# Turning a decoder's input once, unscaled, and keeping it in DRAM for the first residual

## The chip, the core and the metric

One core of a Trainium2 chip runs the kernel. The metric is the device time of one execution in microseconds. Five engines work side by side, each through its own instructions in a fixed order: TensorE (PE: products and transposes into PSUM), VectorE (DVE), ScalarE (ACT), GpSimd (POOL) and SyncE (SP, which issues transfers). They meet by semaphores.

## What is computed

Two decoder layers, for 1024 prompt tokens and 8 sample tokens of 1024 features. The first layer's mixer is gated linear attention (GLA), the second's sliding-window attention; each layer has a squared-ReLU MLP, and each sub-layer is `h = h + post_norm(f(pre_norm(h)))`. What the change touches is the first sub-layer:

```
def rms_norm(x, g):
    return x * rsqrt(mean(x * x, axis=-1) + NORM_EPS) * g
def gla_mixer(x, s0, w_in, w_gate2, b_gate, g_head, w_out):
    q, k, v, r, z = split(x @ w_in)
    log_a = log_sigmoid(z @ w_gate2 + b_gate) / GLA_TAU
    o, s_new = gla_recurrence(q * GLA_DK_HEAD ** -0.5, k, v, log_a, s0)
    return (rms_norm(o, g_head) * silu(r)) @ w_out, s_new
hp = hp + rms_norm(gla_mixer(rms_norm(hp, norm_mix_pre[0]), ...), norm_mix_post[0])
```

The factor `rsqrt(...)` is one number per token, the gain `g` one per feature.

## The kernel before

Activations lie with features on partitions. The tokens form two groups: A (prompt blocks 0 to 3 and the samples, N = 520, in chunks of 256 and 264) and B (blocks 4 to 7, N = 512). Everything but the attention's inner work is a linear layer, cut into jobs: one job is a column tile of 128 of a weight matrix. Weights and activations are split into a high and a low part (fp32r), and a product is three: `wh xh`, `wh xl`, `wl xh` (L217, L219, L221, the tile `psl`). `prep` (L195 to L205) loads a tile in two halves of 256 KB into three staging buffers `wst`, ScalarE casts the high part `wh`, VectorE subtracts for `wl`; it runs one job ahead. `psl` has three PSUM buffers, all else (`aux`) five.

Around the jobs, `Task` objects hold background work (norms, attention, loading); `tick` emits a step of them when so many us of products have gone by. A scheduler then sets each engine's order from the emitted program, by its own estimates, except for instructions kept in program order by `tc.keep_in_program_order`.

`load_x` (L414 to L478) loads the input by blocks of 128 tokens, tokens on partitions: squares and their sum on ScalarE (L438), the factor with one Newton step (L441 to L446, `xss`), the scaling by factor and gain on VectorE (L449; the gain, broadcast over partitions, is loaded at L467), eight transposes on TensorE (L459, `xT`) and the split into the two parts (L289, L290). For group A this runs at the start, with `wz` (the 16 gate columns) and two weight tiles among it; group B's runs as background task `tB`. `gla_part1` then makes `z` and `r` (copied from PSUM at L511 to `sr`), `gla_gate` the decays `eq` and `ek`, `gla_head` the keys, queries and values of a head (`qd` L585, `ki` L589, copy of `vT` L593), `gla_inner` its recurrence. In `gla_inner` the samples' states are updated (L704, `s`, from the product `pkv` L701), split (`sh` on ScalarE, `sl` on VectorE), and multiplied with the queries (L695, `pso`), collected by `so` (L715) and the product of L719.

The residual: `norms` adds, tile by tile, what `residual` gives. `from_scratch` (L353) reads it from `xs`, a DRAM copy that the norm before has written. The first norms use `from_input` (L356 to L373): load 256 KB of the input, four transposes (L364, `pxi`), for A one of the samples (L371, `pxs`), and an addition from PSUM (L366).

## Time and profile before

| | |
|---|---|
| median of 3 runs | 2284.32 us (2284.18 to 2285.45) |
| span of the profiled execution | 2282.3 us |
| TensorE busy | 2255.3 us |
| VectorE busy | 1463.2 us |
| ScalarE busy | 1230.0 us |
| GpSimd busy | 81.7 us |

The span is measured inside the profiled execution, from its first to its last instruction; the runs' times are 2.0 us longer. Busy times are sums over an engine's instructions; an idle engine's row names the instruction or transfer that ended the idle time.

### The profile page before, as it was taken

The page shows a single profiled execution, that of the slowest core. Times are in us where ns is not written, and L with a number is a line of the kernel's source. Part 1 is how long each engine was busy: PE and PEld are TensorE (multiplying, and loading weights), DVE is VectorE, ACT ScalarE, POOL GpSimd, SP SyncE. Part 2 cuts the span into 40 slices and gives each one's busy share as a digit, 9 for nine tenths or more (in the row PEclk, how much of TensorE's full clock was granted, in tenths as well). Part 3 has the DMA queues.
Part 4 walks back from the last instruction along what each step waited for, and adds up shares of the span by engine and source line. Part 5 has one row for each costly group of instructions (what it writes and reads, how often), then busy time and mean ns, then how long its engine had stood idle before and what let it go on. Part 6 is the DMA issues. An engine that isn't in the chain of part 4 may idle for free.

```text
span 2282.3 us, 39657 instructions
## 1 busy us (share of the span) xinstructions
PE 2255.3 (99%) x14764; PEld 2053.8 (90%) x14764; DVE 1463.2 (64%) x3186; ACT 1230.0 (54%) x2614; POOL 81.7 (4%) x121
## 2 busy tenths in 40 slices
...
GB/s 169 128 132 92 105 78 77 126 138 155 93 93 93 90 92 172 97 110 93 79 86 77 103 157 131 131 111 77 75 75 78 93 163 110 171 105 97 93 97 83
DMA packets 413634, 246.75 MB, mean 108 GB/s; under 512 B 17817, under 2 KB 400889, under 8 KB 412641
## 3 DMA queue, kind: packets, MB, share of 16 engines
...
q8 instruction: 116, 1.90, 0.4%
...
## 4 chain that ended last, share of the span: by engine, by line
PE 95%; DVE 2%; DMA 1%; ACT 1%; issue 0%; POOL 0%; ACTq 0%; DVEq 0%; POOLq 0%
PE psl L219 29%; PE psl L217 29%; PE psl L221 29%; PE psc L978 1%; PE ppt L1007 1%; PE po L1018 1%; PE po L1019 1%; PE pP L657 1%; PE pO L684 0%; PE pO L682 0%; PE pxi L364 0%; PE pvt L629 0%; PE patt L633 0%; DMA cm<-const_cmask_dram 0%; DVE nxn L334 0%
## 5 line engine op out<-in xcount | busy, mean ns | idle before, releaser
L217 PE MATMUL psl<-xh,wh 128*128 128x512 f32 (+2 forms) x2784 | 890.8, 320 | 0.7 <-ACT sr L511 0.3
L221 PE MATMUL psl<-xh,wl 128*128 128x512 f32 (+2 forms) x2784 | 886.0, 318 | 1.8 <-DVE xss L445 1.7
L219 PE MATMUL psl<-xl,wh 128*128 128x512 f32 (+2 forms) x2784 | 886.6, 319 | 0.0
L204 ACT CAST wh<-wst 128x512 fp32r<-128x512 f32 x712 | 440.9, 620 | 717.1 <-PE psl L219 629.7
L205 DVE TENSOR_TENSOR wl<-wst,wh 128x512 fp32r<-128x512 f32 x712 | 497.5, 700 | 347.2 <-ACT wh L204 310.9
L221 PEld LDWEIGHTS psl<-xh,wl 128*128 128x128 f32 x2784 | 523.3, 188 | 39.1 <-DVE wl L205 2.4
L217 PEld LDWEIGHTS psl<-xh,wh 128*128 128x128 f32 x2784 | 524.1, 188 | 37.6 <-ACT sr L511 0.6
L219 PEld LDWEIGHTS psl<-xl,wh 128*128 128x128 f32 x2784 | 523.9, 188 | 35.8
L221 PE MATMUL psl<-hh,wl 128*128 128x256 f32 (+2 forms) x1536 | 487.3, 317 | 0.0
L217 PE MATMUL psl<-hh,wh 128*128 128x256 f32 (+1 forms) x1504 | 479.6, 319 | 0.0
L219 PE MATMUL psl<-hl,wh 128*128 128x256 f32 (+1 forms) x1504 | 479.2, 319 | 0.0
L221 PEld LDWEIGHTS psl<-hh,wl 128*128 128x128 f32 x1536 | 288.9, 188 | 20.5
L217 PEld LDWEIGHTS psl<-hh,wh 128*128 128x128 f32 x1504 | 283.0, 188 | 20.8 <-ACT hh L289 0.3
L219 PEld LDWEIGHTS psl<-hl,wh 128*128 128x128 f32 x1504 | 282.7, 188 | 20.7 <-DVE hl L290 0.3
L793 DVE TENSOR_TENSOR yf<-yf,psl 128x256 f32<-128x256 f32 (+1 forms) x344 | 172.4, 502 | 151.7 <-PE psl L221 150.2
L290 DVE TENSOR_TENSOR hl<-rl,hh 128x256 fp32r<-128x256 f32 (+1 forms) x192 | 98.8, 515 | 144.5 <-ACT hh L289 144.4
L780 ACT ACTIVATE rl<-psl 128x256 f32<-128x256 f32 (+1 forms) x192 | 87.1, 454 | 63.1 <-PE psl L221 57.5
L781 ACT ACTIVATE rl<-rl 128x256 f32<-128x256 f32 (+1 forms) x192 | 94.5, 492 | 4.6
L289 ACT CAST hh<-rl 128x256 fp32r<-128x256 f32 (+1 forms) x192 | 92.3, 481 | 4.7
L305 DVE TENSOR_TENSOR nacc<-nacc,nsq 128x520 f32<-128x520 f32 (+1 forms) x99 | 68.6, 693 | 17.3 <-ACT nsq L304 15.0
L992 ACT ACTIVATE pb<-pb,mx 128x256 f32<-128x256 f32 (+1 forms) x128 | 62.2, 487 | 5.7 <-DVE mx L990 4.7
L984 DVE CUSTOM_DVE_ANT_0 pb<-psc,smask 128x256 f32<-128x256 f32 (+1 forms) x128 | 47.8, 401 | 1.2 <-PE psc L978 1.1
...
## 6 DMA issues: line engine op xcount, KB each, us to landing
wst<-in_ffn_w_up_dram SPq DMA_DIRECT2D x256, 256.0 KB
wst<-in_ffn_w_down_dram SPq DMA_DIRECT2D x256, 256.0 KB
...
```

Of the source, the lines that this page charges most:

```text
L204: nc.scalar.copy(out=wh[:, :, :m], in_=st[:, :, :m])
L205: nc.vector.tensor_tensor(out=wl[:, :, :m], in0=st[:, :, :m], in1=r(wh[:, :, :m]), op=ALU.subtract)
L217: nc.tensor.matmul(o, lhsT=wh[:, k % 4, :m], rhs=xh[:, k, c0:c0 + n], start=(k == 0), stop=False)
L219: nc.tensor.matmul(o, lhsT=wh[:, k % 4, :m], rhs=xl[:, k, c0:c0 + n], start=False, stop=False)
L221: nc.tensor.matmul(o, lhsT=wl[:, k % 4, :m], rhs=xh[:, k, c0:c0 + n], start=False, stop=(k == kt - 1))
L289: nc.scalar.copy(out=h, in_=src)
L290: nc.vector.tensor_tensor(out=l, in0=src, in1=r(h), op=ALU.subtract)
L305: nc.vector.tensor_tensor(out=acc, in0=acc, in1=sq, op=ALU.add)
L780: nc.scalar.activation(out=rl, in_=ps, func=AF.Relu)
L781: nc.scalar.activation(out=rl, in_=rl, func=AF.Square)
L793: nc.vector.tensor_tensor(out=o, in0=o, in1=ps, op=ALU.add)
L992: nc.scalar.activation(out=pb[:, i, k0:], in_=pb[:, i, k0:], func=AF.Exp, bias=mx[:, i:i + 1], accum_out=st[:, 2 + i:3 + i])
```

## The change

The input is turned as it is, in pairs of blocks, four PSUM tiles of 128x2x256 to a pair. The gain, now one number per partition (`g1`), is applied as the tiles leave PSUM. Group B multiplies by the factor there too (`rsB`: the factors of 256 tokens on all partitions, by a product of ones with a diagonal matrix `dg` into `prs`). Group A does not: its products with `w_in` are made from the unscaled input, and the factors `rsA` are multiplied afterwards: into `z`, `sr` and `vT` as they leave PSUM, on VectorE, and into `eq` and `ek` on GpSimd, which carries them into queries and keys. `keep` copies each turned tile from PSUM (ScalarE) and writes it to `xs` in DRAM, from ScalarE's queue for A and from GpSimd's for B; `from_input` is gone, and the first norms read their residual from there. `wz` comes in one transfer, the gate's weights later, and several casts and subtractions are kept in program order. Comments were removed as well. The core of the diff, blank lines left out:

```diff
+    g8 = const.tile([KT, P], F32, name="g8")
+    nc.scalar.dma_start(out=g8, in_=n_mix_pre[0].rearrange("(k p) -> k p", p=P))
+    g1 = const.tile([P, KT], F32, name="g1")
+    pg = aux([P, KT], "pg")
+    nc.tensor.transpose(pg, g8, ident[:KT, :KT])
+    nc.vector.tensor_copy(out=g1, in_=pg)
 ...
     def prep_z(w, col0, pin=False):
         wz = gp.tile([P, KT, 2 * RANK], F32R, tag="wz", name="wz", bufs=1)
-        for hf in range(2):
-            st = wpool.tile([P, 4, P], F32, tag="wst", name="wst", bufs=WS)
-            nc.sync.dma_start(out=st[:, :, :RANK], in_=w[hf * 512:hf * 512 + 512, col0:col0 + RANK].rearrange(
+        st = wpool.tile([P, 4, P], F32, tag="wst", name="wst", bufs=WS)
+        st = st.rearrange("p a b -> p (a b)")[:, :KT * RANK].rearrange("p (k m) -> p k m", m=RANK)
+        nc.sync.dma_start(out=st, in_=w[:, col0:col0 + RANK].rearrange("(k p) m -> p k m", p=P))
+        wh, wl = wz[:, :, :RANK], wz[:, :, RANK:]
+        pinned(nc.scalar.copy(out=wh, in_=st), pin)
+        pinned(nc.vector.tensor_tensor(out=wl, in0=st, in1=r(wh), op=ALU.subtract), pin)
         return wz
 ...
-    def from_input(y, g):
-        def add_x(k):
-            xt = npool.tile([P, 4, P], F32, tag="nt", name="nxi", bufs=3)
-            nc.scalar.dma_start(out=xt, in_=x_prompt[0, g.b0 * P:(g.b0 + 4) * P, k * P:(k + 1) * P].rearrange(
-                "(n p) d -> p n d", p=P))
-            pt = aux([P, 4, P], "pxi")
-            for n in range(4):
-                nc.tensor.transpose(pt[:, n, :], xt[:, n, :], ident)
 ...
-                ps = aux([P, NS], "pxs")
-                nc.tensor.transpose(ps, xm, ident[:NS, :NS])
-                nc.vector.tensor_tensor(out=y[:, k, TB:TB + NS], in0=y[:, k, TB:TB + NS], in1=ps, op=ALU.add)
-        return add_x
-    def norms(g, gpost, gpre, box, residual=from_scratch):
+    def norms(g, gpost, gpre, box):
         y = g.y
-        yield from post_norm(y, g, gpost, residual(y, g))
 ...
-    gbc, xtk = scr[:, 0:D], scr[:, 3 * D:4 * D]
+    rsA, rsB, xsm = scr[:, 0:NMAX], scr[:, NMAX:NMAX + 256], scr[:, NMAX + 256:D]
+    xtk = [scr[:, D:2 * D], scr[:, 3 * D:4 * D]]
 ...
-    def load_x(g, box, tiles, early=None):
 ...
-            for hf in range(2):
-                c = slice(hf * 512, hf * 512 + 512)
-                nc.vector.scalar_tensor_tensor(out=t[:, c], in0=t[:, c], scalar=y, in1=gbc[:rows, c],
-                                               op0=ALU.mult, op1=ALU.mult)
 ...
+    def load_x(g, h, l, pair, tiles):
+        own = g.i == 0
+        c0 = pair * 256
+        ns = g.ns if pair == 1 else 0
+        def pin(ins):
+            return pinned(ins, own)
+        for i in range(2):
+            row = (g.b0 + 2 * pair + i) * P
+            nc.sync.dma_start(out=tiles[i], in_=x_prompt[0, row:row + P, :])
+        if ns:
+            nc.sync.dma_start(out=tiles[2][:NS], in_=x_sample[:, 0, :])
+        yield YD
+        ss = gp.tile([P, 12], F32, tag="xss", name="xss", bufs=4)
+        if ns:
+            nc.gpsimd.memset(ss, 1.0)
+        n = 3 if ns else 2
+        def squares(i):
+            rows = P if i < 2 else NS
             jk = gp.tile([P, D], F32, tag="Sp", name="xsq", bufs=1)
+            sq = nc.scalar.activation(out=jk[:rows], in_=tiles[i][:rows], func=AF.Square,
+                                      accum_out=ss[:rows, i:i + 1])
+            if i:
+                pin(sq)
+        def factors():
+            ms, y, u = ss[:, 3:3 + n], ss[:, 6:6 + n], ss[:, 9:9 + n]
+            nc.vector.tensor_scalar(out=ms, in0=ss[:, 0:n], scalar1=1.0 / D, scalar2=EPS, op0=ALU.mult, op1=ALU.add)
             nc.scalar.activation(out=y, in_=ms, func=AF.Ln)
             nc.scalar.activation(out=y, in_=y, func=AF.Exp, scale=-0.5)
+            nc.vector.tensor_tensor(out=u, in0=y, in1=ms, op=ALU.mult)
+            nc.vector.tensor_tensor(out=u, in0=u, in1=y, op=ALU.mult)
             nc.vector.tensor_scalar(out=u, in0=u, scalar1=-0.5, scalar2=1.5, op0=ALU.mult, op1=ALU.add)
             nc.vector.tensor_tensor(out=y, in0=y, in1=u, op=ALU.mult)
+            N = 256 + ns
+            dg = nt(N, "dg")
+            for i in range(2):
+                nc.vector.tensor_scalar_mul(dg[:, i * P:(i + 1) * P], ident, y[:, i:i + 1])
+            pt = prs
+            nc.tensor.matmul(pt[:, :256], lhsT=ones, rhs=dg[:, :256], start=True, stop=True)
+            if ns:
+                nc.vector.tensor_scalar_mul(dg[:NS, 256:N], ident[:NS, :NS], y[:NS, 2:3])
+                nc.tensor.matmul(pt[:, 256:N], lhsT=ones[:NS], rhs=dg[:NS, 256:N], start=True, stop=True)
+            nc.scalar.copy(out=rsA[:, c0:c0 + N] if own else rsB, in_=pt[:, :N])
+        if ns:
+            pt = aux([P, KT, NS], "xTs")
+            for k in range(KT):
+                nc.tensor.transpose(pt[:, k, :], tiles[2][:NS, k * P:(k + 1) * P], ident[:NS, :NS])
+            t = xsm[:, 0:KT * NS].rearrange("p (k s) -> p k s", s=NS)
+            u = xsm[:, KT * NS:2 * KT * NS].rearrange("p (k s) -> p k s", s=NS)
+            nc.vector.tensor_copy(out=u, in_=pt)
+            nc.gpsimd.dma_start(out=xs[g.i][:, :, TB:TB + NS], in_=u)
+            nc.vector.tensor_tensor(out=t, in0=u, in1=g1.unsqueeze(2).to_broadcast([P, KT, NS]), op=ALU.mult)
+            split(h[:, :, TB:TB + NS], l[:, :, TB:TB + NS], t)
+        prs = aux([P, 512], "prs")
+        squares(0)
+        if not own:
+            squares(1)
+            factors()
+            yield YD
+        raw = []
+        def keep(k, pt):
+            t = nt(512, "xr").rearrange("p (k t) -> p k t", t=256)
+            pin(nc.scalar.copy(out=t, in_=pt))
+            (nc.scalar if own else nc.gpsimd).dma_start(out=xs[g.i][:, k:k + 2, c0:c0 + 256], in_=t)
+        for k in range(0, KT, 2):
+            pt = aux([P, 2, 256], "xT")
+            for i in range(2):
+                for q in range(2):
+                    nc.tensor.transpose(pt[:, q, i * P:(i + 1) * P], tiles[i][:, (k + q) * P:(k + q + 1) * P], ident)
+            for q in range(2):
+                hk, lk, g_ = h[:, k + q, c0:c0 + 256], l[:, k + q, c0:c0 + 256], g1[:, k + q:k + q + 1]
+                if own:
+                    pin(nc.scalar.activation(out=hk, in_=pt[:, q, :], func=AF.Copy, scale=g_))
+                    pin(nc.vector.scalar_tensor_tensor(out=lk, in0=pt[:, q, :], scalar=g_, in1=r(hk),
+                                                       op0=ALU.mult, op1=ALU.subtract))
+                else:
+                    t = nt(256, "nxn")
+                    nc.vector.scalar_tensor_tensor(out=t, in0=pt[:, q, :], scalar=g_, in1=rsB,
+                                                   op0=ALU.mult, op1=ALU.mult)
+                    split(hk, lk, t)
+            if own:
+                raw.append((k, pt))
+            else:
+                keep(k, pt)
+            yield YN
+        if own:
+            squares(1)
+        if ns:
+            squares(2)
+        if own:
+            factors()
+        for k, pt in raw:
+            keep(k, pt)
+    def load_b():
+        h, l = new_xn(B)
+        xB.append((h, l))
+        for pair in range(2):
+            yield from load_x(B, h, l, pair, xtk)
+    def gla_part1(g, x, needs, early=None):
         cell = {}
 
 ...
             z = g.z3[:, c0:c0 + n]
+            if g.rs is not None:
+                t = nt(n, "zt")[:2 * RANK]
+                nc.vector.tensor_tensor(out=t, in0=ps, in1=g.rs[:2 * RANK, c0:c0 + n], op=ALU.mult)
+                ps = t
             nc.scalar.copy(out=z[0:32], in_=ps)
             nc.scalar.copy(out=z[64:96], in_=ps)
 ...
         def ev_r(t):
-            return lambda ps, c0, n: nc.scalar.copy(out=g.sr[:, t, c0:c0 + n], in_=ps)
+            return lambda ps, c0, n: plain(g.sr[:, t, c0:c0 + n], ps, c0, n)
+        def plain(out, ps, c0, n):
+            if g.rs is None:
+                nc.scalar.copy(out=out, in_=ps)
+            else:
+                nc.vector.tensor_tensor(out=out, in0=ps, in1=g.rs[:, c0:c0 + n], op=ALU.mult)
+        g.plain = plain
+        if early is None:
             lin(w_in[0], 0, 3072, x, g, ev_z, m=RANK, needs=needs, pre=pre_z)
         else:
             t0 = 2
             pre_z()
+            tiles = [x0[:, n * D:(n + 1) * D] for n in range(4)] + [xtk[1]]
+            h, l = new_xn(A)
+            early.append((h, l))
+            first, second = load_x(A, h, l, 0, tiles[:2]), load_x(A, h, l, 1, tiles[2:])
+            next(first)
+            wz = prep_z(w_in[0], 3072, True)
+            next(first)
+            next(first)
+            w0 = prep(w_in[0], 0, KT, 2048, P, pin=True)
+            next(second)
+            for _ in first:
+                pass
+            w1 = prep(w_in[0], 0, KT, 2048 + P, P)
             g.sr = new_big(g, "sr")
-            for c in g.chunks:
-                mms_z(wz[0], x, [c], ev_z)
-                for t in range(t0):
-                    mms(wz[1 + t], KT, P, x, [c], ev_r(t))
+            for i, c in enumerate(g.chunks):
+                mms_z(wz, x, [c], ev_z)
+                mms(w0, KT, P, x, [c], ev_r(0))
+                if i == 0:
+                    for _ in second:
+                        pass
+                mms(w1, KT, P, x, [c], ev_r(1))
+            load_gate()
             load_params()
 ...
+        if g.rs is not None:
+            for t in (eq, ek):
+                nc.gpsimd.tensor_tensor(out=t[:, :N], in0=t[:, :N], in1=g.rs[:, :N], op=ALU.mult)
         g.gate[hd] = (eq, ek, av)
 ...
         def ev_v(t):
-            return lambda ps, c0, n: nc.scalar.copy(out=cell["vT"][:, t, c0:c0 + n], in_=ps)
+            return lambda ps, c0, n: g.plain(cell["vT"][:, t, c0:c0 + n], ps, c0, n)
 ...
     A.inner, B.inner = [], []
     x0 = new_big(A, "x0").rearrange("p k n -> p (k n)")
-    wA = []
-    tA = Task(load_x(A, xA, [x0[:, n * D:(n + 1) * D] for n in range(4)] + [xtk], {
-        2: lambda: wA.append(prep_z(w_in[0], 3072, True)),
-        3: lambda: wA.append(prep(w_in[0], 0, KT, 2048, P)),
-        4: lambda: wA.append(prep(w_in[0], 0, KT, 2048 + P, P))}), 1)
-    need(tA)
-    load_gate()
-    tB = add(load_x(B, xB, [xtk] * 4), SLB)
-    for g, box, ts in ((A, xA, [tA]), (B, xB, [tB])):
+    A.rs, B.rs = rsA, None
+    tB = add(load_b(), SLB)
 ...
     jobs, nA = after(out_proj(A, w_out[0], lambda: oA[-1], A.inner + [tSA]),
-                     norms(A, gains["mpost", 0], gains["fpre", 0], xA, from_input), S0)
 ...
     gla_stack.close()
-    nB = add(norms(B, gains["mpost", 0], gains["fpre", 0], xB, from_input), S1)
```

Where instructions stand now. First ScalarE at the start, before; `xss` are the norm's factors, `xT` the turned input, `wh` a weight half.

```order
L438 ACTIVATE xsq_118,xss_119<-x00_111 128x1024
L442 ACTIVATE xss_119<-xss_119 128x1
L443 ACTIVATE xss_119<-xss_119 128x1
L438 ACTIVATE xsq_130,xss_131<-x00_111 128x1024
L442 ACTIVATE xss_131<-xss_131 128x1
L443 ACTIVATE xss_131<-xss_131 128x1
L289 CAST xh0_112<-xT_141 128x4x128
```

Three small ScalarE steps stand before the first turned tile is split. After the change, `wh_152` to `wh_217` being the four halves of the first two weight tiles, `scr1` the buffer that holds `rsA`:

```order
L493 ACTIVATE xh0_119<-xT_165,g1_89 128x256
L215 CAST wh_211<-wst_209 128x512
L493 ACTIVATE xh0_119<-xT_165,g1_89 128x256
L493 ACTIVATE xh0_119<-xT_174,g1_89 128x256
L215 CAST wh_217<-wst_215 128x512
L493 ACTIVATE xh0_119<-xT_174,g1_89 128x256
L436 ACTIVATE xsq_183,xss_128<-x00_117 128x1024
L436 ACTIVATE xsq_287,xss_270<-x00_117 128x1024
L444 ACTIVATE xss_128<-xss_128 128x2
L445 ACTIVATE xss_128<-xss_128 128x2
L460 COPY scr1_105<-prs_129 128x256
L482 COPY xr_197<-xT_132 128x512
```

Squares, logarithm and exponential, which stood ahead of the first turned tile, now stand behind the casts of the first pair and of the fourth weight half, but for the first square; the copy of `rsA` follows them.

TensorE in the first head of group A, before: the samples' products `pso` stand between products `psl` of a linear layer.

```order
L217 MATMUL psl_1619<-xh0_112,wh_1609 128x256
L219 MATMUL psl_1619<-xl0_113,wh_1609 128x256
L221 MATMUL psl_1619<-xh0_112,wl_1610 128x256
L217 MATMUL psl_1619<-xh0_112,wh_1609 128x256
L695 MATMUL pso_1442<-sh_1540,qm_103 16x256
L701 MATMUL pkv_1570<-v3_102,k3_101 128x256 x2
L219 MATMUL psl_1619<-xl0_113,wh_1609 128x256
L221 MATMUL psl_1619<-xh0_112,wl_1610 128x256
L217 MATMUL psl_1619<-xh0_112,wh_1609 128x256
L695 MATMUL pso_1442<-sl_1541,qm_103 8x256
```

After the change no such `psl` is among them. TensorE at the same place after the change, up to the next `psl`:

```order
L764 MATMUL pso_1541<-sh_1657,qm_109 16x256
L764 MATMUL pso_1541<-sl_1658,qm_109 8x256
L764 MATMUL pso_1541<-sh_1664,qm_109 16x256
L764 MATMUL pso_1541<-sl_1665,qm_109 8x256
L764 MATMUL pso_1541<-sh_1675,qm_109 16x256
L764 MATMUL pso_1541<-sl_1676,qm_109 8x256
L764 MATMUL pso_1541<-sl_1683,qm_109 8x256
L764 MATMUL pso_1541<-sh_1682,qm_109 16x256
L788 MATMUL pso2_1693<-fold_110,so_1691 128x8 x2
L228 MATMUL psl_1594<-xh0_119,wh_1558 128x264
L230 MATMUL psl_1594<-xl0_120,wh_1558 128x264
L232 MATMUL psl_1594<-xh0_119,wl_1559 128x264
```

The `psl` that stood between have moved: the chain's last rows stand together, and the next `psl` behind `pso2`.

VectorE at this place before (`qd` takes queries out of PSUM and so frees a buffer of `psl`; `Sp` and `stmp` are the prompt's state):

```order
L585 SCALAR_TENSOR_TENSOR qd_1366<-psl_1369,eq_1213 128x256
L663 TENSOR_SCALAR Sp_1325<-stmp_1333,av_658 128x256
L661 TENSOR_TENSOR stmp_1339<-pP_1336,Sp_1325 128x256
L205 TENSOR_TENSOR wl_1610<-wst_1607,wh_1609 128x512
L663 TENSOR_SCALAR Sp_1325<-stmp_1339,av_658 128x256
L585 SCALAR_TENSOR_TENSOR qd_1366<-psl_1395,eq_1213 128x264
```

Here `qd` follows at once on the prompt's state steps. After the change, where `so` collects the samples' products and `nxn` is a scaled tile of group B's input:

```order
L616 COPY mid_1771<-ta_1620 128x4
L624 COPY av_1774<-la_1621 128x8
L617 TENSOR_TENSOR ta_1620<-ta_1620,mid_1771 128x512
L784 COPY so_1691<-pso_1541 16x256
L498 SCALAR_TENSOR_TENSOR nxn_1132<-xT_1127,g1_89,scr1_105 128x256
L498 SCALAR_TENSOR_TENSOR nxn_1136<-xT_1127,g1_89,scr1_105 128x256
L654 SCALAR_TENSOR_TENSOR qd_1465<-psl_1468,eq_1310 128x256
L298 TENSOR_TENSOR xl1_505<-nxn_1132,xh1_504 128x256
```

`qd` of the next head's first chunk, which stood ahead of the sample chain, now stands behind its end and behind two `nxn`.

## Rows read from the trace of the kernel before

**Rows 1.** Busy time of each engine, share of the span, instructions (the page).
```profile
PE 2255.3 (99%) x14764; PEld 2053.8 (90%) x14764; DVE 1463.2 (64%) x3186; ACT 1230.0 (54%) x2614; POOL 81.7 (4%) x121
```
**Rows 2.** Windows: length, busy us of PE, PEld, DVE, ACT, POOL, clock, DMA.
```profile
0.00:20.00 20.00, 8.96 (x54) 7.25 (x54) 11.37 (x30) 12.38 (x29) 17.94 (x39) 1.00 0.83 198
20.00:40.00 20.00, 16.55 (x128) 14.85 (x129) 12.42 (x39) 9.73 (x27) 0.05 (x1) 1.00 0.54 151
...
140.00:160.00 20.00, 19.17 (x157) 18.58 (x156) 18.96 (x41) 10.82 (x20) 1.55 (x3) 1.00 0.32 86
```
**Rows 3.** TensorE's waits in the first 41 us: total us, times, longest.
```profile
PE psl L221 <- DVE xss L445: 1.7, 2, 1.5
```
**Rows 4.** Timeline of TensorE at group A's residual: start, length [idle before].
```profile
445.13 0.39 PE L221 MATMUL psl<-xh,wl 128*128 128x512 f32 x1
...
447.80 0.40 PE L219 MATMUL psl<-xl,wh 128*128 128x512 f32 x1
...
463.71 0.39 PE L217 MATMUL psl<-xh,wh 128*128 128x512 f32 x1
...
464.91 0.40 PE L221 MATMUL psl<-xh,wl 128*128 128x512 f32 x1
```
**Rows 5.** Timeline of TensorE at the first step of group B's residual.
```profile
524.95 0.28 PE L221 MATMUL psl<-hh,wl 128*128 128x264 f32 x1
525.07 0.60 PE L364 MATMUL pxi<-ident,nxi 128*128 128x128 f32 x4
...
525.63 0.28 PE L219 MATMUL psl<-hl,wh 128*128 128x256 f32 x1
```
**Rows 6.** Groups of instructions, 119.9 to 127.95 us: busy, mean ns, idle before.
```profile
L221 PE MATMUL psl<-xh,wl 128*128 128x256 f32 (+1 forms) x14 | 4.0, 282 | 0.0
...
L704 DVE SCALAR_TENSOR_TENSOR s<-s,av,pkv 128x256 f32<-128x256 f32 x6 | 2.6, 475 | 0.0
L290 DVE TENSOR_TENSOR sl<-s,sh 128x256 fp32r<-128x256 f32 x6 | 2.3, 418 | 0.1
```
**Rows 7.** Timeline of VectorE around the end of the sample chain.
```profile
120.26 0.48 DVE L704 SCALAR_TENSOR_TENSOR s<-s,av,pkv 128x256 f32<-128x256 f32 x1
...
127.43 0.39 DVE L715 COPY so<-pso 16x256 f32<-16x256 f32 x1
127.75 0.15 DVE L550 COPY mid<-ta 128x4 f32<-128x4 f32 x1
...
128.61 0.68 DVE L551 TENSOR_TENSOR ta<-ta,mid 128x512 f32<-128x512 f32 x1
```
**Rows 8.** Timeline of ScalarE at the start.
```profile
22.96 0.62 ACT L204 CAST wh<-wst 128x512 fp32r<-128x512 f32 x1 [1.90 <-DMA wst<-in_gla_w_in_dram]
...
33.81 1.06 ACT L438 ACTIVATE xsq<-scr 128x1024 f32<-128x1024 f32 x1 [1.85 <-DMA scr<-in_x_prompt_dram]
...
39.26 0.62 ACT L204 CAST wh<-wst 128x512 fp32r<-128x512 f32 x1 [2.15 <-DMA wst<-in_gla_w_in_dram]
```
**Rows 9.** Timeline of SyncE's transfers at the start.
```profile
36.22 3.45 SPq L195 DMA_DIRECT2D wst<-in_gla_w_in_dram  x3
```
**Rows 10.** Groups of the whole span: the residual's additions.
```profile
L366 DVE TENSOR_TENSOR y<-y,pxi 128x512 f32<-128x512 f32 x16 | 10.9, 684 | 8.4 <-PE pxi L364 8.2
L353 DVE TENSOR_TENSOR y<-y,nx 128x520 f32<-128x520 f32 (+1 forms) x16 | 10.9, 688 | 0.0
```
**Rows 11.** Timeline of TensorE around f32 products of 256 columns.
```profile
104.93 1.89 PE L657 MATMUL pP<-vtok,ktok 128*128 128x256 f32 x8
106.46 0.47 PE L221 MATMUL psl<-xh,wl 128*128 128x256 f32 x1
```
**Rows 12.** Timeline of GpSimd in the second layer.
```profile
948.70 1.82 POOL L867 TENSOR_TENSOR qsw<-qsw,sin 128x520 f32<-128x520 f32 x1 [4.59 <-DMA qsw<-kr]
```
**Rows 13.** Timeline of VectorE at the same place.
```profile
947.74 0.69 DVE L205 TENSOR_TENSOR wl<-wst,wh 128x512 fp32r<-128x512 f32 x1 [1.86 <-ACT wh L204]
...
949.28 1.79 DVE L205 TENSOR_TENSOR wl<-wst,wh 128x512 fp32r<-128x512 f32 x1
```

85 lines of the change are left out of this document (16 added, 69 removed).

## The prediction

> **What bounds the kernel now.** I read the busy times of the engines first: TensorE is busy for 2255.3 us of the 2282.3 us of the profiled span [rows 1], so the kernel is one stream of products, and a change is worth what it takes out of that stream, less the holes that it puts into it. Next I read the windows, to see where there are holes now [rows 2]. TensorE is busy for 8.96 us of the first 20 and for 16.55 us of the next 20: 14.5 us of holes at the start, then none to speak of (19.17 of 20 in 140 to 160 us). In that last window VectorE is busy for 18.96 of 20 us; there it is as loaded as TensorE. One of the waits of the start is for the factors of the norm, `xss` [rows 3]. Then I read the places that the change touches: the residual of the first norm, where the input is turned a second time [rows 4, 5]; the chain of sample products in the first head [rows 6, 7]; and the landing of the first weights [rows 8, 9].
>
> **Removed: the residual's transposes.** 64 `pxi` and 8 `pxs` leave TensorE. For group A the first step lies between the products of 445.13 and 447.80 us [rows 4]: 2.67 us, in which two products of 512 columns would take 0.47 (one of 264 columns takes 0.12, 524.95 to 525.07 [rows 5]); 2.2 us are left, part of it a wait for the load. Six further steps are like that of 463.71 to 464.91 us: 1.20 less 0.47, 0.73 us each. A last `pxs` alone is about half a step, 0.35 us. Together 6.95 us. For group B four `pxi` stand in the stream eight times: 524.95 to 525.63 us less two products of 0.12, 0.44 us each, 3.5 us. So **-10.5 us**. The addition on VectorE stays: with the residual from DRAM (L353) it takes 688 ns and waited for nothing, with the turned one (L366) 684 ns, and 8.2 us in all for `pxi` [rows 10]. The loads of the residual are asked for ahead, as in the other norms. I take **+1 us** (0 to 2) for holes at the end of A's norm that the transposes covered until now: VectorE's additions there still take their 16 x 0.69 us, and the next layer's products wait for the last.
>
> **Added: factors of group B.** Two products of ones with a diagonal (f32, 256 columns). Eight records, four such products, stand between 104.93 and 106.46 us [rows 11], 0.38 us each; two are 0.8 us. A turned tile of B now leaves PSUM only after two VectorE steps that need the factors, and a ScalarE copy, where it was one cast and one subtraction; the transposes behind it wait in TensorE's stream. The nearest row is the wait of 1.7 us for `xss` [rows 3]; I take 1 us (0 to 3). Together **+1.8 us**.
>
> **Moved: the chain of sample products.** This is the dearest part, and only the order shows it. Before, VectorE worked nearly without a gap from the state update of 120.26 us to the copy `so` that ends at 127.82 [rows 7], 7.6 us: updates of 475 ns, splits of 418 ns [rows 6], and steps of the gate between. Under that cover TensorE ran 14 triples of `psl` products [rows 6], 42 x 0.12 = 5.0 us, between the `pso` products that wait for the chain. In the changed order all the `pso` of the chain stand in a row, and the next `psl` (the second chunk of head 1's keys) behind them. It would wait in any case: its PSUM buffer is freed by `qd`, which stands on VectorE behind `so` and two `nxn` of group B. The chain is not shorter: 7.6 us, plus three gate steps that now stand ahead of `so` (0.15 + 0.15 + 0.68 [rows 7]), plus two `nxn` and `qd` behind it (3 x 0.42, taken from the splits of 256 columns): 9.9 us. TensorE has in it 16 `pso`, 6 `pkv` and two `pso2`, some 24 x 0.12 = 3 us. The hole is **+6.9 us**, where before there was next to none. It is at least 4 us (the 5.0 us of products that lose their place, less a microsecond of small waits that end with them) and at most 9, with a further block of B in the way.
>
> **Moved: the start.** The gain's broadcast load and the scaling ahead of the transposes go, so TensorE can turn the input as soon as it lands, some microseconds earlier. But a new wait ends the chain. The first pair's products are multiplied by `rsA`, and ScalarE's row for `rsA` stands behind the cast of the fourth half weight tile. The transfer of that tile can only be issued when the first of three staging buffers is free again, by my count at 11 to 13 us (landing of the first half, cast, subtraction). A transfer of 256 KB took from 36.22 us, its issue [rows 9], to 39.26, the cast that waited for it [rows 8]: 3 us; at 22.96 us a cast waited 1.90 us for one, though asked for much earlier. So I have the cast at 15 to 17 us. Behind it come two squares (1.06 us each [rows 8], and their sums), logarithm, exponential, five small VectorE steps, two diagonals, the ones product and a copy, some 6 us with the handovers: `rsA` at 21 to 23 us. Then the second pair: on each half of a PSUM tile ScalarE's scaled copy and VectorE's remainder take turns, about 0.42 us each and two handovers, 1.0 us for each of eight: 30 to 31 us. The second chunk's products, two `psl` (24 x 0.12 each) and a `psz` (16 x 0.12), are 7.7 us: the stream is full from 38 to 41 us on. Before, it was full from 39.5 us [rows 2], the holes ending in the second window, with 0.9 us of B's transposes already done, which makes 38.6. The count gives -0.6 to +2.4 us; since it is a chain of some thirty handovers of which I can price only a few, I take its upper end, **+2.5 us** (-1.5 to +8).
>
> **Off the path.** The copies of A's `sr` and `vT` move from ScalarE to VectorE, 32 of 0.42 us; most fall where VectorE has room. The eight multiplications of `eq` and `ek` on GpSimd come ahead of their use. Such a multiplication of 128x520 took 1.82 us [rows 12], and a VectorE subtraction that started beside it 1.79 us, where another took 0.69 [rows 13]: each can cost VectorE 1.1 us, all eight 8.8 us, at places where little waits for it. I take **+0.5 us** for both. The gate's weights come later and `wz` in one transfer instead of two: nothing, since no late product hangs on them.
>
> The Trainium skill ("SBUF — State Buffer", section "Who interferes with whom") says that a VectorE instruction with two SBUF inputs and a GpSimd instruction that reads SBUF take turns at one port pair, the later one fully blocked. The trace agrees, with the 1.79 us of rows 13. Were every one of the eight to block a subtraction that TensorE waits for, the sum would be 8.8 us for it instead of 0.5.
>
> **The sum.** -10.5 + 1 + 1.8 + 6.9 + 2.5 + 0.5 = +2.2 us. The profiled span is 2282.3 us and the median 2284.32, 2.0 us above; I carry that over and forecast **2286.5 us**. A measurement of this kernel can tell 0.2% (4.6 us) from no change, so "same" is 2279.7 to 2288.9 us.
>
> **Rivals.**
> - *The saving stays* (2277.1 us). The start gains 1.5 us, because nothing waits for the scaling any more; the chain costs its lower 4 us, B's factors 0.8, the rest nothing: -10.5 - 1.5 + 4 + 0.8 = -7.2. For it speaks that the holes of the first 20 us are the largest of the kernel, 11 us [rows 2], and the change starts TensorE earlier in them; against it that the order of TensorE around the chain is fixed.
> - *The factors come late: slower than before* (2291.5 us). If the fourth half tile lands at 20 to 22 us instead of 15 to 17, all behind it moves by the same 5 us: -10.5 + 1 + 1.8 + 6.9 + 7.5 + 0.5 = +7.2. It passes the bound of "same" from a landing of about 18.5 us on. For it: ScalarE's waits for such transfers in rows 8, and the input of the second pair asked for in front of it. Against it: much of what competed for transfers before, the broadcast of 512 KB, is gone.
> - *GpSimd blocks VectorE* (2290.5 us). Two of the four heads have their multiplications where VectorE is as busy as in 140 to 160 us [rows 2]; half of the 8.8 us on the path makes +2.2 + 4 = +6.2 us. Against it: `eq` and `ek` of a head are used a good while later.
> - *It doesn't do what it says*: the 72 transposes are gone from the order; no chance for that.
>
> **Chances.** Forecast 0.48, saving stays 0.18, late factors 0.22, blocking 0.12. The terms' bounds spread the forecast over 2281 to 2291, so 0.06 of it lies above 2288.9. Faster: 0.18, the first rival. Slower: 0.22 + 0.12 + 0.06 = 0.40. Same: 0.42. The range goes from just under the first rival, 2276.5, to 2296, the late factors with the chain at its upper end; 2 in 10 are left out.
>
> **What would show it.** A full TensorE without `pxi` in 444 to 468 and 524 to 548 us: the -10.5 us. A wait of TensorE for `so` or `qd` of 5 us or more around 120 us: the chain; a full window there is the first rival. The end of the holes at the start: near 41 us for the forecast, near 46 for late factors, with ScalarE's wait for the fourth half tile as their cause. VectorE subtractions of 1.8 us beside GpSimd's rows, and TensorE waiting for `wl` or `qd` behind them: the third. I am wrong in kind if new holes stand behind 250 us, where I see none but those at A's norm, or if the granted clock, 1.00 in all of rows 2, falls in the new wait at the start.

## The result, and the profile after

| | time, median (runs) | profiled execution: span, mean granted clock |
|---|---|---|
| before, beside it | 2284.89 us (4: 2284.18 to 2285.46) | 2282.3 us, 0.999 |
| after | 2318.64 us (4: 2314.00 to 2319.61) | 2312.2 us, 0.991 |

The changed kernel is slower: ratio 1.0141, 95% interval 1.0126 to 1.0155. The profiled execution of after is the fastest of its four (2314.00 us), that of before lies 0.6 us under its median, so the traces show 29.9 us of the 33.8 between the medians. The busy times (the page of after, as [rows 1]):

```profile
PE 2265.1 (98%) x14703; PEld 2057.9 (89%) x14703; DVE 1478.3 (64%) x3219; ACT 1232.1 (53%) x2604; POOL 100.1 (4%) x139
```

TensorE has 61 instructions fewer and is busy 9.8 us longer. Part of why stands in the windows of after (columns as in [rows 2]; the last but two is the granted clock):

```profile
0.00:20.00 20.00, 10.13 (x59) 8.47 (x60) 6.18 (x14) 8.84 (x18) 18.10 (x40) 1.00 1.04 225
20.00:40.00 20.00, 12.69 (x66) 8.12 (x64) 7.15 (x23) 10.47 (x25) 0.90 (x1) 0.67 0.50 125
...
80.00:100.00 20.00, 16.85 (x116) 16.36 (x115) 7.77 (x22) 10.41 (x17) 0.75 (x1) 0.83 0.47 144
140.00:160.00 20.00, 16.38 (x111) 14.55 (x112) 17.93 (x44) 10.77 (x25) 6.26 (x12) 0.83 0.49 156
492.00:496.00 4.00, 0.49 (x3) 0.07 (x1) 0.71 (x2) 1.01 (x2) 0.00 (x0) 0.83 0.79 214
496.00:502.00 6.00, 4.70 (x14) 3.93 (x15) 4.40 (x10) 4.02 (x10) 0.00 (x0) 0.55 0.33 98
```

In the first 20 us TensorE does more than before, 10.13 us for 8.96; in the next 20 less, 12.69 for 16.55, and at a mean clock of 0.67, that is, much of it at the lower of its two levels (1.2 instead of 2.4 GHz). Then there are holes where before had none: at 80 to 100 us, in the first head's chain, and at 492 us. The first of these windows in before:

```profile
80.00:100.00 20.00, 20.00 (x170) 20.00 (x169) 13.23 (x28) 13.79 (x26) 0.00 (x0) 1.00 0.41 118
```

The waits of TensorE over the whole span (total, times, longest) name them; the wait for `g` at the very start ends before any product could begin:

```profile
PE pg L129 <- DMA g<-in_norm_mix_pre_dram: 4.9, 1, 4.9
PE pnorm L322 <- ACT nah L297: 4.8, 1, 4.8
PE prs L456 <- DVE dg L454: 4.7, 2, 3.1
PE psz L255 <- DVE zt L532: 4.5, 1, 4.5
PE pso L764 <- DVE sl L298: 4.1, 5, 1.6
...
PE pso L764 <- ACT sh L297: 1.6, 3, 0.8
```

To say where the time goes, I compared the two timelines product by product: both kernels run the same 4352 `psl` products with a low half of the weights, and the start of the n-th after less that of the n-th before is the lag at that point. The column head is the start in before. Background work stands between these products, so a lag can also be work done early, and a gain work put off.

```
lag in us at        60.0  80.3 114.1 124.6 419.4 469.4 498.1 569.8 2272.1
after               13.6  19.9  20.2  29.4  28.8  22.7  29.4  27.2  29.5
e1 gate on VectorE  13.3  14.9  15.2  15.1  16.8  10.9  17.3  14.9  16.9
e2 room             7.8   10.9  11.2  21.0  20.8  14.8  21.8  18.8  20.2
e3 pieces           13.6  18.9  19.2  29.5  30.1  26.7  26.9  27.7  30.8
e4 nothing kept     5.4   5.9   6.2   15.0  14.5  17.4  17.4  17.4  18.0
e5 = e1 + e2        8.1   8.1   8.5   8.0   8.3   3.5   11.1  9.5   11.2
e7 no copy          12.9  13.2  13.5  13.4  14.5  8.4   15.1  13.4  15.4
e9 = e5 + pieces A  8.1   8.1   8.4   8.0   9.4   7.8   8.0   5.2   7.1
e10 = e9 + turns    4.0   3.1   4.5   4.4   4.3   3.3   3.4   3.0   4.7
e11 = e5 + fillers  6.2   6.2   6.6   6.1   7.1   1.9   9.5   6.7   8.1
e12 B alone         -0.1  -1.0  3.5   3.4   6.5   8.0   8.0   5.3   6.5
e13 e10, B as before 0.8  5.7   4.3   2.5   6.9   4.2   4.4   4.4   7.0
e14 e13, A not kept 1.0   1.0   2.7   2.8   4.4   4.8   4.9   4.9   6.8
e15 e10, ones later 2.5   3.4   -5.3  -6.4  31.6  28.5  28.6  26.8  29.0
e16 e10, one write  3.1   2.3   3.7   3.6   3.4   -1.1  5.8   3.4   4.7
e17 e10, A not kept -0.3  -1.1  1.2   1.1   2.7   5.0   5.1   2.7   3.6
```

Each row is one profiled execution: after's lies 4.6 us under its median, e3's 2.6 and e10's 2.9 above theirs, the others within 2.1.

So after loses 13.6 us at the start, 7.2 between 70 and 80 us of before's time, 9.2 in the sample chain; it wins 6.1 at A's residual, loses 6.7 right behind it, wins 2.2 at B's; the rest (+1.1) is spread.

**The start.** At the product that before starts at 20 us, after is 4.8 us ahead; at 31 us it is 9.6 behind. ScalarE, VectorE and TensorE in the timelines of after (start, length, [idle before <- releaser]):

```profile
18.64 0.62 ACT L215 CAST wh<-wst 128x512 fp32r<-128x512 f32 x1 [3.23 <-DMA wst<-in_gla_w_in_dram]
...
24.80 0.37 ACT L460 COPY scr<-prs 128x256 f32<-128x256 f32 x1 [2.57 <-PE prs L456]
...
31.85 0.59 ACT L482 COPY xr<-xT 128x512 f32<-128x512 f32 x1 [3.25 <-DMA xs<-xr]
```
```profile
32.93 0.41 DVE L532 TENSOR_TENSOR zt<-psz,scr 32x256 f32<-32x256 f32 x1 [3.81 <-DMA xs<-xr]
...
37.18 0.88 DVE L494 SCALAR_TENSOR_TENSOR xl<-xT,g,xh 128x256 fp32r<-128x256 f32 x2 [0.54 <-ACT xh L493]
```
```profile
33.48 0.40 PE L255 MATMUL psz<-xh,wz 128*32 128x264 f32 x1 [4.55 <-DVE zt L532]
```

The fourth half tile is cast at 18.64 us, `rsA` is copied at 24.80. Behind it stand the four copies `xr` for the residual: they share three buffers with `zt`, each is free again only when its write to DRAM has landed, and so both the fourth copy (3.25 us) and `zt` (3.81 us) wait for a write, and TensorE for `zt`. Then `xh` and `xl` of the second pair take turns until 39 us. At 45 us the lag is 9.5; in the other 4.1 us of the 13.6 B's first pair is scaled and turned, with a wait of 1.57 us for `dg`.

**80 to 99 us.** Of after: ScalarE waits for a weight tile, and at the end TensorE for the scaled identity `dg`, which stands on VectorE behind the remainder of that tile; at the lower clock the products that follow start 0.21 us apart instead of 0.13:

```profile
87.89 0.62 ACT L215 CAST wh<-wst 128x512 fp32r<-128x512 f32 x1 [5.52 <-DMA wst<-in_gla_w_in_dram]
```
```profile
88.88 0.29 PE L228 MATMUL psl<-xh,wh 128*128 128x256 f32 x1
89.01 0.28 PE L230 MATMUL psl<-xl,wh 128*128 128x256 f32 x1
92.43 1.22 PE L456 MATMUL prs<-dg,ones 128*128 128x256 f32 x2 [3.15 <-DVE dg L454]
...
94.52 0.41 PE L228 MATMUL psl<-xh,wh 128*128 128x256 f32 x1
94.73 0.41 PE L230 MATMUL psl<-xl,wh 128*128 128x256 f32 x1
```

**The sample chain**, answering [rows 6]: TensorE's groups from 138 to 146.9 us (busy, mean ns, idle before). There is no `psl` among them:

```profile
L764 PE MATMUL pso<-sh,qm 128*16 128x256 f32 x8 | 2.4, 301 | 1.5 <-DVE la L605 1.0 <-ACT sh L297 0.5
L764 PE MATMUL pso<-sl,qm 128*8 128x256 f32 x8 | 2.3, 294 | 2.4 <-DVE sl L298 2.4
L788 PE MATMUL pso<-fold,so 16*128 16x8 f32 x4 | 1.0, 360 | 0.5 <-DVE so L784 0.5
L770 PE MATMUL pkv<-v,k 72*128 72x256 f32 x4 | 0.8, 293 | 0.0
```

These waits are 4.4 us together (the rest of the `pso` waits in the list above stands in later heads). The last `psl` ahead of the chain starts at 136.79 us, the next one at 146.97; it and the 28 short products between them would take 3.5 us at 0.12 each, which leaves a hole of some 6.7 us.

**A's residual**, answering [rows 4]: no transposes, but a hole. GpSimd's row, ScalarE's, and TensorE's, which names `nah`, though `nah` itself stands behind the cast that waits for a weight tile:

```profile
485.82 0.54 POOL L367 DMA_DIRECT2D xs<-y  x1 [15.21 <-DMA wst<-in_gla_w_out_dram]
```
```profile
494.64 0.62 ACT L215 CAST wh<-wst 128x512 fp32r<-128x512 f32 x1 [5.66 <-DMA wst<-in_gla_w_out_dram]
```
```profile
497.30 0.81 PE L322 MATMUL pnorm<-nah,ones_r 128*128 128x256 f32 x2 [4.81 <-ACT nah L297]
```

The write of the new residual, 2 MB, lands 7.9 us after its issue, and the last weight tiles of the layer were asked for around it, up to 497.59 us (transfers of after, 480 to 497 us, and SyncE's issues):

```profile
xs<-y POOLq DMA_DIRECT2D x1, 2080.0 KB, 7.9
```
```profile
461.71 35.88 SPq L206 DMA_DIRECT2D wst<-in_gla_w_out_dram  x13
```

Before, the same write was issued at 467.83 us, after the last of these tiles had been asked for (up to 467.55 us):

```profile
441.25 26.30 SPq L195 DMA_DIRECT2D wst<-in_gla_w_out_dram  x8
```
```profile
467.83 0.54 POOL L378 DMA_DIRECT2D xs<-y  x1 [26.05 <-issue]
```

### The profile page after: what moved, and what is told of

Read it like the earlier page. It is cut to its first block, busy times and chain, and to the rows that moved or that the text cites. A ratio compares the mean times of both kernels' runs of the same rounds, so it can differ in the third digit from the quotient of the medians.

```text
span 2312.2 us, 39592 instructions
## 1 busy us (share of the span) xinstructions
PE 2265.1 (98%) x14703; PEld 2057.9 (89%) x14703; DVE 1478.3 (64%) x3219; ACT 1232.1 (53%) x2604; POOL 100.1 (4%) x139
## 4 chain that ended last, share of the span: by engine, by line
PE 91%; DVE 3%; DMA 2%; ACT 2%; issue 1%; ACTq 0%; DVEq 0%; SPq 0%
PE psl L228 28%; PE psl L230 28%; PE psl L232 28%; PE psc L1047 1%; PE ppt L1076 1%; PE po L1087 1%; PE po L1088 1%; PE pP L726 1%; DMA wst<-in_gla_w_out_dram 1%; PE pO L753 0%; PE pO L751 0%; DMA xs<-xr 0%; DVE wl L216 0%; DMA wst<-in_gla_w_in_dram 0%; ACT wh L215 0%
```

## The experiments

Times are medians, ratios are against runs of the kernel before on the same chip (medians of 2284.2 to 2285.9 us). The first four take one suspected cost away each.

**e1**: `eq` and `ek` are multiplied on VectorE.

```diff
-                nc.gpsimd.tensor_tensor(out=t[:, :N], in0=t[:, :N], in1=g.rs[:, :N], op=ALU.mult)
+                nc.vector.tensor_tensor(out=t[:, :N], in0=t[:, :N], in1=g.rs[:, :N], op=ALU.mult)
```

> The changed kernel with one line altered: the factors are multiplied into eq and ek on VectorE, not on GpSimd. In its order the samples' products pso of the first head stand between psl again. Theory (the scheduler gave GpSimd's slow multiplication a late end, put qd behind the sample chain, and so took the psl out of it): the 9.2 us that the changed kernel loses between 114 and 125 us of before's time shrink to about 1, total 2318.6 - 8 = about 2310 us. Rival (the hole comes from VectorE's larger load, whoever multiplies): eight more VectorE steps of 0.69 us make it longer, 2319 to 2324 us.

2301.78 us, ratio 1.0077 (1.0062 to 1.0092): 16.9 us less than after, twice the forecast. The lags show where: 9 us are won in the chain, as the theory had it, and 5 at 70 to 80 us, which it hadn't. In e1's trace the `pso` stand between `psl` products again and wait for nothing (TensorE's groups, 136 to 147 us):

```profile
L230 PE MATMUL psl<-xl,wh 128*128 128x256 f32 (+1 forms) x23 | 6.6, 287 | 0.0
...
L764 PE MATMUL pso<-sh,qm 128*16 128x256 f32 x8 | 2.2, 282 | 0.0
L764 PE MATMUL pso<-sl,qm 128*8 128x256 f32 x8 | 2.2, 280 | 0.0
```

The order around the chain is another one than in after. The edit changes an order, and the order is worth more than the step.

**e2**: room of their own for four of the eight copies at the start.

```diff
-            t = nt(512, "xr").rearrange("p (k t) -> p k t", t=256)
+            if own and k >= 4:
+                t = scr[:, 2 * D + (k - 4) * 256:2 * D + (k - 2) * 256].rearrange("p (k t) -> p k t", t=256)
+            else:
+                t = nt(512, "xr").rearrange("p (k t) -> p k t", t=256)
```

> The changed kernel with four of group A's eight residual copies xr in another, idle buffer, so that three shared buffers no longer wait for writes to DRAM. Theory (the 3.25 us wait of ScalarE and the 3.8 us wait of VectorE at 28 to 33 us are a link of the chain of the start): the second chunk comes 3 to 4 us earlier, and the half clock ends earlier too: 2318.6 - 4 to 5 = about 2314 us. Rival (the second pair's alternation of ScalarE and VectorE sets the end anyway): within 1 us of 2318.6.

2303.80 us, 1.0087 (1.0069 to 1.0106). That is 10 us under the forecast. The start wins 5.8 us, more than the 3 to 4 that the waits for `xs<-xr` had promised; another 3 are won at 70 to 80 us, which I had not expected. The chain costs 9.8 as in after.

**e3**: the residual is written chunk by chunk, in all norms.

```diff
         nc.vector.tensor_tensor(out=y[:, k, :], in0=y[:, k, :], in1=xt, op=ALU.add)
+        nc.gpsimd.dma_start(out=xs[g.i][:, k, :], in_=y[:, k, :])
...
-        nc.gpsimd.dma_start(out=xs[g.i], in_=y)
```

> The changed kernel, but each norm writes its residual to DRAM in eight pieces, one behind each addition, not in one transfer of 2 MB at its end. Theory (that transfer now falls between the loads of the last w_out tiles, 5.66 us of waiting, and the halved clock that follows costs 3.4 us more): the hole at 492 us goes, total 2318.6 - 5 to 8 = about 2312 us. Rival (the norm's end simply lacks the work that the transposes were): the hole stays, within 1 us of 2318.6.

2312.66 us, 1.0127 (1.0104 to 1.0150). No loss at 498 us any more, but at 469 us only 3.4 are won instead of 6.1: TensorE waits 2.5 us there for a high part, and as long for `yf` in a later norm. The write in one piece makes the hole; the pieces, issued in all norms, cost as much elsewhere: at the end e3's trace lags 30.8 us and after's 29.5. The median is 6 us lower, but the two intervals overlap.

**e4**: nothing is kept; both residuals are read from the input and turned again, as before (`from_input` back, `keep` out).

> The changed kernel with the old residual: the input loaded and turned a second time in the first norms, nothing kept in DRAM at the start (no xr copies, no writes). It leaves the unscaled turning, the late factors and the chain. Theory (the losses are separate): start 4 us shorter, chain as before, the hole at 492 us gone, 10.5 us of transposes back: 2318.6 - 4 - 7 + 10.5 = about 2318 us. Rival (the residual kept in DRAM is the cause of most of the loss): 2290 to 2300 us.

2301.24 us, 1.0073 (1.0057 to 1.0088), the rival's side. Keeping costs 8 us at the start and nearly all of the 7 at 70 to 80 us, and brings less than this at the norms. The chain costs 8.8 us here too, without any write of a kept tile to DRAM.

**e5**: e1 and e2 together.

> The changed kernel with both edits of the first and the second experiment: factors multiplied into eq and ek on VectorE, and four of the eight xr copies in an idle buffer. Theory (two separate losses, each with its own cure: 14.3 us up to 125 us for the one, 5.8 us at the start for the other): 2318.6 - 16 - 6 to 9 = 2292 to 2297 us. Rival (both cure the same, the late end of the start): no better than 2301 us, the faster of the two.

2294.86 us, 1.0043 (1.0028 to 1.0058), inside the expectation; the hole at A's norm is whole (3.5 to 11.1).

**e6**: ten products whose results nobody reads, in a PSUM tile of their own, between the second pair's transposes and the products that follow.

> The changed kernel with ten products whose result nobody reads, on TensorE between the transposes of group A's second pair and the second chunk (3.8 us of work into a hole of 4.5 us). Theory (the halved clock of 30.4 to 44.1 us follows from the hole, and its cost is what the products between 39 and 44 us lose, 2 to 3 us): granted clock 1.00 there, 2318.6 - 2 to 3 = about 2316 us. Rival (the clock falls whatever TensorE does there, or it costs nothing because the chain of copies sets the pace): 2318 to 2320 us.

2314.19 us, 1.0121 (1.0104 to 1.0138). The fillers themselves waited 4.6 us for a PSUM buffer; the run says nothing about the clock. **e11** asks again, on e5, in a tile that is there anyway:

```diff
+        if own and pair == 1:
+            for i in range(10):
+                nc.tensor.matmul(prs[:, 272:512], lhsT=ident, rhs=rsA[:, 0:240], start=True, stop=True)
```

> The kernel of e5 (2294.9 us) with ten products of 240 columns more, whose results nobody reads, on TensorE between the last transposes of x's second pair and the products that follow, in a corner of a PSUM tile that is there anyway. It tells what the granted clock of 0.5 costs at the start (kernel after: 30.4 to 44.1 us). Theory (the fall follows the gaps, the products behind them are slower for it): the stretch at 0.5 gets shorter, 1.5 to 3 us less than e5, about 2292 to 2293.5 us. Rival (the products at half clock wait for operands anyway): 2295 us or, by the fillers' own time, up to 2297 us.

2293.70 us, 1.0042 (1.0027 to 1.0057); e5 had 1.0043. The window of 20 to 40 us, of e5 and of e11:

```profile
20.00:40.00 20.00, 15.87 (x80) 11.01 (x80) 7.62 (x24) 12.69 (x30) 0.90 (x1) 0.67 0.58 144
```
```profile
20.00:40.00 20.00, 16.43 (x116) 14.06 (x114) 8.94 (x29) 13.09 (x31) 0.95 (x2) 1.00 0.61 154
```

The clock is at 1.00 throughout, and the lag at 60 us falls from 8.1 to 6.2. So the lower clock costs some 2 us of the lag at the start, and most of the lag is waiting. The median is 1.2 us lower, which the intervals can't tell from nothing.

**e7**: the copy of the value cache, 1 MB, is left out (so all but the newest row of that output aren't written).

> The changed kernel without the 1 MB copy of the samples' value cache from DRAM to DRAM (rows 0 to 126 of that output are left out). Theory (at 82 to 88 us that copy, started at 78.6 us, holds up a weight half for 5.5 us, and VectorE's diagonals for prs stand behind it: 3.15 us of hole, then a halved clock): the 7.2 us lost between 80 and 99 us shrink to 1 or 2, 2318.6 - 5 = about 2313 us. Rival (the eight writes of the turned input alone load the queues enough): the hole stays, 2318 us.

2301.44 us, 1.0071 (1.0056 to 1.0086), much better than either theory. The hole at 80 to 99 us is gone:

```profile
80.00:100.00 20.00, 20.00 (x167) 19.69 (x166) 13.54 (x36) 15.14 (x27) 2.29 (x4) 1.00 0.41 111
```

ScalarE's longest wait for a weight tile there is 0.6 us instead of 5.5. But the chain's 9 us are gone too, with the multiplications still on GpSimd: again the order came out with `pso` between `psl`. With e1 this says that the order decides the chain, not the engine that multiplies, and the other runs bear it out: in after, e2, e3, e4 and e6 no `psl` stands among the chain's sixteen `pso`, and the lag grows by 8.8 to 10.3 us between 114.1 and 124.6 us; in the thirteen other runs some do, and it doesn't grow. For the hole it leaves two causes open, the megabyte less on the DMA engines and the new order around it.

**e8**: the parameters of the second half are loaded as rows and turned, instead of element by element.

> The changed kernel with the norms' gains and biases loaded as rows and turned on TensorE, instead of 4 bytes at a time from 8 to 19 us. Theory (these loads fill the queues and delay the third and fourth weight half, for which ScalarE waited 2.75 and 3.23 us; everything of the start stands behind them): the fourth half lands 4 us earlier, at about 14 us, and the second chunk comes as much earlier: start 13.6 to 9 us, total about 2313 us, less if the order of the sample chain changes as well. Rival (the landing is set by the bytes of the inputs and weights): the fourth half lands at 18 us as before.

2340.20 us, 1.0241 (1.0226 to 1.0257). The new transposes stand in TensorE's stream and wait for their loads (4.3, 4.2 and 2.3 us for three of the parameters): TensorE is busy for 7.0 of the 30 us from 100 to 130, and the lag grows from 14.1 us (at 80.3 us of before) to 54.8 (at 114.1). That is the edit's own loss. It doesn't tell whether these loads delay the weights: the 1 MB copy of the key cache, which had stood behind them on GpSimd, is issued at 9.02 us instead of 19.24, and the fourth half tile is cast later, at 20.95 us.

**e9**: e5, with the pieces of e3 in A's first norm alone. **e10**: e9, and `xh` and `xl` alternate over two PSUM tiles:

```diff
+                for q in range(2):
+                    for j, pt in enumerate(pts):
+                        pin(nc.scalar.activation(out=h[:, k + 2 * j + q, c0:c0 + 256], in_=pt[:, q, :], ...))
+                    for j, pt in enumerate(pts):
+                        pin(nc.vector.scalar_tensor_tensor(out=l[:, k + 2 * j + q, c0:c0 + 256], ...))
```

> The kernel after with the multiplication of the sample chain on VectorE, room of its own for four of the eight copies at the start (both as in e5, 2294.9 us), and the residual written chunk by chunk behind its additions in group A's first norm alone. Theory (the hole of 7.6 us in A's last w_out tiles comes from the 2 MB write that lies between the weight loads): the hole goes and nothing takes its place, about 2288 us. Rival (the pieces share the queues with the loads for as long, so the gain is given back in the norm itself, as in e3): 2293 to 2295 us.

> The kernel of e9, and at the start ScalarE's high parts and VectorE's low parts alternate over two PSUM tiles, so that the two engines don't wait for each other at every half tile (L493, L494: 1.42 us per tile of two halves in the kernel after). Theory (this chain feeds the second chunk of group A's first products): 2 to 3 us less than e9, about 2285 to 2286 us. Rival (the weight casts and the third DMA of x set the start): the same as e9 within 1 us.

e9: 2290.09 us (10 runs), 1.0024 (1.0015 to 1.0033); e10: 2285.83 us (10 runs), 1.0005 (0.9996 to 1.0015). e9 lies between theory and rival: the hole at 498 us is gone, but A's residual wins only 1.6 us where e5 had won 4.8, so that some 4 of 7.6 us are left as a gain. e10 is where the theory had it: its start wins 4.1 us. VectorE's eight remainders of the second pair now take 3.7 us, where e9 needed 5.8, and they begin 1.6 us earlier, since the first pair alternates too (first and last of e9, then all of e10):

```profile
30.11 0.48 DVE L500 SCALAR_TENSOR_TENSOR xl<-xT,g,xh 128x256 fp32r<-128x256 f32 x1 [1.24 <-ACT xh L499]
...
35.39 0.48 DVE L500 SCALAR_TENSOR_TENSOR xl<-xT,g,xh 128x256 fp32r<-128x256 f32 x1 [0.54 <-ACT xh L499]
```
```profile
28.52 0.88 DVE L508 SCALAR_TENSOR_TENSOR xl<-xT,g,xh 128x256 fp32r<-128x256 f32 x2 [1.24 <-ACT xh L504]
29.55 1.66 DVE L508 SCALAR_TENSOR_TENSOR xl<-xT,g,xh 128x256 fp32r<-128x256 f32 x4 [0.15 <-ACT xh L504]
31.36 0.88 DVE L508 SCALAR_TENSOR_TENSOR xl<-xT,g,xh 128x256 fp32r<-128x256 f32 x2 [0.15 <-ACT xh L504]
```

Four edits, none of which touches what the change computes, have taken back 32.8 of the 33.8 us.

**e12**: the kernel before with group B's half of the change alone.

> The kernel before with the change made in group B alone: B's input is turned once, unscaled, and kept in DRAM as its residual; group A is as before. Theory (B's half of the change costs 5 us of the hole at 80 to 99 us, where its writes meet the weight loads, and brings 2 to 3.5 us at B's norm; the start, the sample chain and the hole at 492 us belong to A's half): 2282 to 2288 us. Rival (the hole at 82 to 99 us belongs to A's lag at the start): 2281 to 2283 us, below before.

2293.06 us, 1.0043 (1.0026 to 1.0060), above both theory and rival. B's norm brings 2.7 us (8.0 to 5.3), as the removed transposes should; the lag grows by 4 us behind 80 us, where TensorE waits for `dg` again,

```profile
85.93 0.70 PE L536 MATMUL prs<-dg,ones 128*128 128x256 f32 x2 [2.39 <-DVE dg L534]
```

and by 4.6 more up to 469 us. The clock is 1.00 throughout: it isn't needed for such a loss.

**e13**: e10 with group B as before. **e14**: e13 with A's residual from the input too. **e15**: e10 with B's ones products 10 us of products later. **e16**: e10 with A's residual written in one piece, behind the norm's second part.

> The kernel of e10 (2285.8 us) with group B as in the kernel before: B's blocks are scaled, turned one by one, and its residual is read from the input again and turned a second time. Theory (from e12: B's half of the change costs more than the 2.8 us that it brings at B's norm): 2281 to 2284 us. Rival (B's costs came from the order around it, which e10 no longer has; its trace shows no wait of TensorE from 75 to 105 us): 2287 to 2289 us, the saving at B's norm lost.

> The kernel of e13 with group A's residual too read from the input and turned a second time in A's first norm, and nothing kept in DRAM at the start. What is left of the change: A's input turned unscaled and the reciprocals behind the products. Theory (the copies for the kept residual cost up to 3 us at the start, and the turning again costs A's norm 1 us more than the write in pieces): 1 to 2 us less than e13. Rival (the copies have room of their own now and cost nothing, the turning again costs what it cost before): 1 to 5 us more than e13.

> The kernel of e10 (2285.8 us) with group B's ones products (the row tile that spreads the reciprocals of two blocks over all partitions, line 459) put 10 us of matrix products behind the scaled identity that they read, instead of right behind it. Theory (where the scaled identity comes late, TensorE stands at this product: 3.2 us in the kernel after, 2.4 us in e12): 1 to 2 us less than e10. Rival (in e10 the identity is in time): the same as e10 within 1 us.

> The kernel of e10 (2285.8 us) with A's residual written as one piece of 2 MB again, but after the second part of the norm, so that it starts when all of the layer's weight tiles have been loaded. Theory (the pieces of e10 still lie between the weight loads: TensorE waits 2.4 us for a high and 2.0 us for low parts at 432 to 500 us): 3 to 4 us less than e10, about 2282 us. Rival (the write meets the loads of the next layer just as well): the same as e10 or up to 3 us more.

e13: 2291.77 us, 1.0029 (1.0019 to 1.0038), above both. Taking B's half back makes e10 6 us slower, where adding it to before had cost 7: the parts don't add. Its new hole stands at 60 to 80 us (TensorE busy 16.70 of 20), where B's blocks are scaled and turned one by one.

e14: 2290.28 us, 1.0022 (1.0013 to 1.0032), 1.5 us under e13, as the theory had it, but the two intervals overlap.

e15: 2313.27 us, 1.0119 (1.0102 to 1.0136), 27 us over e10, against both theory and rival. The step put off pushed the background work behind it past the products that had covered it; e15 is 6.4 us ahead at 124.6 us, and then works the rest off bare:

```profile
200.00:210.00 10.00, 5.78 (x37) 5.28 (x36) 3.51 (x10) 3.92 (x9) 0.73 (x1) 0.83 0.47 157
...
240.00:250.00 10.00, 5.02 (x28) 3.19 (x26) 5.14 (x14) 3.86 (x9) 1.43 (x2) 0.85 0.71 213
250.00:260.00 10.00, 8.06 (x47) 7.60 (x47) 7.04 (x16) 4.27 (x11) 0.00 (x0) 0.81 0.04 14
260.00:270.00 10.00, 7.89 (x31) 6.99 (x32) 7.06 (x14) 5.26 (x8) 0.00 (x0) 0.66 0.00 0
```

e16: 2289.79 us, 1.0019 (1.0010 to 1.0029), above both. The edit didn't delay the write: GpSimd has nothing else to do and issues it as soon as `y` is complete, in the middle of the last weight loads, and the hole is back as it was in after (GpSimd's, ScalarE's and TensorE's rows of e16):

```profile
462.03 0.54 POOL L373 DMA_DIRECT2D xs<-y  x1 [17.89 <-DMA wst<-in_gla_w_out_dram]
```
```profile
470.88 0.62 ACT L215 CAST wh<-wst 128x512 fp32r<-128x512 f32 x1 [5.69 <-DMA wst<-in_gla_w_out_dram]
```
```profile
473.54 0.80 PE L322 MATMUL pnorm<-nah,ones_r 128*128 128x256 f32 x2 [4.84 <-ACT nah L297]
```

Against e10, which differs only in writing pieces, this is a clean pair: one write, lag from -1.1 to 5.8; pieces, from 3.3 to 3.4. The hole belongs to the 2 MB, and the pieces give back most of what they save.

All runs together show what sets the hole. Where A's residual is kept and written in one piece (after, e1, e2, e5, e6, e7, e8, e11, e16), the lag grows by 6.5 to 8.3 us between 469.4 and 498.1 us; in pieces (e3, e9, e10, e13, e15), by 0.1 or 0.2; where A's input is turned again and the residual written in one piece (e4, e12, e14, e17), by 0.1 at most. In these last four, as in before, the write is issued 0.2 to 0.3 us after the last of the layer's loads; in after, e5 and e16 nearly 12 us ahead of that load.

**e17**: e10 with A's residual from the input, nothing of A kept.

> The kernel of e10 (2285.8 us) with group A's residual read from the input and turned a second time in A's first norm, and nothing of A kept in DRAM at the start; group B as in the kernel after (turned once, kept). Theory (at the start the copies cost 3 us, as e14 against e13 has it in the products of 60 us; B's half brings what e13 lost against e10; at A's norm the write in pieces and the turning again cost about the same): 2282 to 2284 us, below the kernel before. Rival (the two groups' halves don't add, as e12 and e13 have it: the order of the work beside the products decides, and it comes out by chance): 2286 to 2291 us.

2286.32 us (11 runs), 1.0008 (0.9999 to 1.0017), at the near end of the rival's range. The start is 0.3 us ahead of before at 60 us, with TensorE busy 17.19 of 20 us at full clock in its second window:

```profile
20.00:40.00 20.00, 17.19 (x129) 14.31 (x128) 13.06 (x43) 13.59 (x32) 0.00 (x0) 1.00 0.58 138
```

What it wins there it loses again between 80 and 420 us (lag -1.1 to 2.7) and at A's residual, where `pxi` waits 2.6 us for its load. No version beat the kernel before; e10 and e17 are level with it.

## Why the prediction was wrong

The forecast was 2286.5 us, within 2276.5 to 2296; the kernel takes 2318.6. Three steps failed: at the start I left out the kept copies and the buffers that they hold, at A's norm the 2 MB write, and at B's factors a weight half that comes late. Point by point:

- **The residual's transposes** (-10.5): the size was mostly right, but for A the place as a whole loses. A wins 6.1 us for 6.95, B 2.2 for 3.5 (2.7 in e12). The +1 us for holes at A's norm was 6.7: I looked at VectorE's additions there, and not at GpSimd's write behind them. The transposes had delayed `y`, and with it the 2 MB write, to just after the last weight load; without them the write comes before it. This is an order of two transfers that the trace of before shows (467.83 us against the last loads), and that I didn't look up. e16 against e10 shows that the hole is the write's, and e4, e12, e14 and e17 that with the transposes the write comes late enough. The Trainium skill ("DMA: Bandwidth & Descriptors", section "Issuing engines are not separate DMA queues") says that transfers of all issuing engines run on the same 16 DMA engines and interleave. The trace agrees: GpSimd's write, 7.9 us to its landing, and SyncE's 256-KB loads, for which ScalarE waited 5.66 us.
- **Factors of B** (+1.8): the place costs 7.2 us in after and 4 in e12. The named wait, TensorE in front of `prs`, was there, so the step was the right one; but it came twice (1.57 and 3.15 us), 4.7 us for my 1 and over its bound of 3. What was missing is what lies ahead of the second: a weight half for which ScalarE waits 5.5 us, and the lower clock for the products behind it. Which of the writes made the tile late is open: room at the start (e2), nothing kept (e4), no cache copy (e7) and another order (e1) each shrink the hole.
- **The sample chain** (+6.9, 4 to 9): the mechanism was right and the size too: a hole of some 6.7 us, of which the named waits make 4.4. The lag's 9.2 hold besides, by my estimate, 1.4 us of some 12 products behind it at the lower clock (0.22 us apart instead of 0.12) and about 1 us of sample work that before does later: at 130 us the lag has grown by 8.1. But I took the order as given by the change; e1, e5 and e7 show that a small edit elsewhere flips it.
- **The start** (+2.5, -1.5 to +8): 13.6, the largest miss. The count up to `rsA` was late by 2 to 4 us (cast at 18.64 us where I had 15 to 17, `rsA` at 24.80 where I had 21 to 23), which is the rival of the late factors, at its very bound of 18.5. What broke the count comes behind it: the second pair is split at 39.08 us, where I had 30 to 31. I left out the eight copies `xr` and the buffers they hold until their writes have landed, although the first of them stands in ScalarE's order right behind the copy of `rsA`; e2 gives 5.8 us for four of them, e4 gives 8.2 for all. The turns of ScalarE and VectorE were not the failure: I had 1.0 us for each half tile, and they took 0.71 (1.42 us for a tile of two halves); alternating over two tiles wins 4.1 all the same (e10).
- **GpSimd** (+0.5): the lock is there. In after a subtraction beside the multiplications took 2.01 us,

```profile
149.90 1.32 POOL L636 TENSOR_TENSOR eq<-eq,scr 128x520 f32<-128x520 f32 x1
```
```profile
150.76 2.01 DVE L298 TENSOR_TENSOR xl<-nxn,xh 128x256 fp32r<-128x256 f32 x1 [1.15 <-ACT xh L297]
```

  where the same form took 0.42 at 148.85, and TensorE had no wait for it. The term stands; e7, which leaves the multiplications on GpSimd, wins the chain's 9 us as e1 does, so that these came from the order and not from this lock.
- **The signs**: of the two for being wrong in kind, the falling clock at the start came; the large hole behind 250 us is at A's norm, the place that I had excepted, but it is 6.7 us for my 1. A wait of 5 us or more for `so` or `qd` didn't come: TensorE waits six times in the chain, 1.6 us at the longest. And the holes of the second chunk end at 40.11 us, near my 41, while the lag there is 9.6 us: the end of the holes doesn't tell how much work is already done.

In short, by the traces: -10.5 was about -8.3, and +12.7 of costs were some 38: 13.6 for 2.5, 7.2 for 1.8, 9.2 for 6.9, 6.7 for 1, and 1 spread over the rest. Left open: why B's half alone costs 7 us on before and its removal 6 us on e10. The lags show the places, but each of the two kernels has another order of background work, and no run held that order fixed.
